# The order of experts, the last scatters and the last column half in a two-layer transformer kernel

## The chip, the cores and the metric

The kernel runs on one core of one Trainium2 chip. The metric is the device time of one execution in microseconds (us); times of the kernel before are the median of three runs. Five engines take part: TensorE (PE in the rows, PEld for its weight loads), VectorE (DVE), ScalarE (ACT), GpSimd (POOL) and SyncE (SP), whose queue issues the loads of weights.

## What is computed

Two transformer layers over 256 tokens of width 1024, in fp32. The first has a latent attention and a dense feed-forward part, the second a sparse attention and a mixture of eight experts. The change touches the mixture and the last layer norm alone:

```python
def moe_swiglu(x, w_router, w_gate, w_up, w_down):      # cut
    logits = (xt @ w_router).astype(jnp.float32)
    top_val, top_idx = lax.top_k(logits, TOP_K)         # 2 of 8 experts per token
    wts = jax.nn.softmax(top_val, -1)
    ...
        xb = xt[toks]                                   # tokens of expert e
        h = jax.nn.silu(xb @ w_gate[e]) * (xb @ w_up[e])    # 1024 -> 3584
        return (h @ w_down[e]) * wr[:, None]                # 3584 -> 1024
    ...
    y = jnp.zeros_like(xt).at[row_tok].add(out.reshape(R, D))

x = layer_norm(alpha * x + f, ln_ffn_g[i], ln_ffn_b[i])
```

Every expert's three matrices are 3 x 1024 x 3584 fp32 numbers, 44.04 MB; all eight are read, 352 MB.

## The kernel before

**Experts and their order.** Expert 0 of the weights is always done first, since its loads start before the router's choice is known. `arrange()` ranks the other seven by their number of tokens (rank 1 has the most), and the constant `turn` says which rank is done at which place: before, places 0 to 7 take ranks 0, 7, 1, 6, 2, 5, 3, 4. `PLAIN` lists the places that are done plainly: at most 64 tokens, weights used in fp32 as they landed. The other three places, of ranks 1 to 3, take up to 128 tokens; there each weight chunk is split by ScalarE (L128) and VectorE (L131) into a high and a low fp32r part, and each product is three fp32r matmuls. A place with more tokens than its limit has a second pass at the end (L1857 on), which is left out when its counter is zero.

**Steps.** Place 0 has steps of 512, 2048 and 1024 hidden columns, the others of 2048 and 1536. In `run()`, for each step: the gate products (L1622, banks `pa`), the first half of the down products of the step before (L1622, banks `pb`), the up products, and the rest of those down products. Transposes of the hidden rows (L1554), the gathering of the next expert's tokens (L1530) and the scatters of the last expert (L1716, L1717, and the weighted sum into `y` on VectorE, L1719) are put between chunks from a queue `fq`.

**Chunks and buffers.** Weights come in chunks of 1 MiB (0.75 MiB in gate and up steps of 1536 columns), each with one or two DMAs on SyncE's queue, in the order in which they are used. An expert has 42 MiB. `seq()` (L421 on) writes out by hand which buffer each chunk goes to: after the first 22 loads the buffers raw0 to raw4, R0, xTh, xTl, x3Th, xna, s2, x3Tl and lng are taken in rotation. R1 to R4 are in it too, until eight keys before ("mg", 2, 0, 0), the first gate chunk of place 2; then they hold the split parts (`rings`, four half chunks of each part). lng leaves the rotation at ("mg", 7, 0, 0), as it takes the norm's gains then. A load is issued when its buffer's last chunk has been used (plain) or split (the others).

**The end.** Place 7's last two down chunks are cut by output columns, `down_tail(at, 0)` and `down_tail(at, 1)`, each with two DMAs of half a MiB. `end()` does half 0, evacuates its bank with `outs` (ScalarE L482, VectorE L483: a high and a low part), puts the scatters of half 0 into `fq`, does half 1, whose `fill` calls take them from there, evacuates it, and does the rest of scatters, squares (L507), means (L511), gains (L520), roots (L515, L516, GpSimd L493) and outputs (L523), with four output DMAs on SyncE (L1817).

Of the kernel before, what the change touches and what calls it, by code (L numbers as in the profile page):

```python
# [20 lines left out]
E = 8  # L21
FE = 3584
FF = 2816
PLAIN = 0, 1, 3, 5, 7


def body(tc, a, out, tap=None, upto=9):
# [31 lines left out]
    HL, NR = 5, 5  # L59
# [221 lines left out]
    fq = deque()  # L281
# [138 lines left out]
    def seq():  # L420

        at = {f"raw{i}": n for i, n in enumerate((2, 3, 5, 6, 7))}
        at.update({z: first.index(z) for z in ("xTh", "xTl", "xna", "lng", "s2", "x3Tl")})
        at.update({i: first.index(R[i]) for i in range(HL)})

        at["x3Th"] = keys.index(("md", 0, 2, 0))

        until = dict.fromkeys(range(1, HL), keys.index(("mg", 2, 0, 0)) - 8)

        until["lng"] = keys.index(("mg", E - 1, 0, 0))  # L430
        yield from first
        n = len(first)
        while True:
            z = min((z for z in at if n < until.get(z, 9999)), key=at.get)
            at[z] = n
            n += 1
            yield R[z] if z in range(HL) else "raw" if z[:3] == "raw" else z
# [76 lines left out]
    def ln_rstd(sm):  # L514
        dve.tensor_scalar(sm[:, 7:8], sm[:, 3:4], sm[:, 4:5], 1.0 / D, op0=ALU.add, op1=ALU.mult)  # L515
        dve.tensor_scalar(sm[:, 7:8], sm[:, 7:8], sm[:, 6:7], LN_EPS, op0=ALU.subtract, op1=ALU.add)  # L516
        rpow(sm[:, 8:9], sm[:, 7:8])
# [53 lines left out]
    p = pT()  # L571
# [1124 lines left out]
    def down_tail(at, i):  # L1696

        e, j, G, hT, acc, gen = at
        key = "md", e, j, i, "tail"
        w = raw_of(*key)  # L1700
        for m in range(2):
            for q in range(2):
                mm(acc[i][64 * q:64 * q + 64], hT[m - 2][:, 64 * q:64 * q + 64], w[2 * m + q], False, m == 1)
            fill(2)
        used(*key)

    def outs(acc, hf):
        oo = four(F32R)
        oo = oo[:, :512], oo[:, 512:]
        evac2(*oo, acc[hf])  # L1710
        return oo

    def scatter(e, oo, ohT, hf, t, sums=None):
        c = slice(hf * 512, hf * 512 + 512)
        p = pT()
        pe.matmul(p, ohT[:, t, :], oo[hf][0], start=True, stop=False)  # L1716
        pe.matmul(p, ohT[:, t, :], oo[hf][1], start=False, stop=True)  # L1717
        y = ys[0]
        dve.scalar_tensor_tensor(y[:, t, c], p, by[0][:, 2 + t, e:e + 1], y[:, t, c], op0=ALU.mult, op1=ALU.add,  # L1719
                                 accum_out=sums[t][:, hf:hf + 1] if sums is not None else None)  # L1720

    def run(todo, G, at, gen=(), end=None):


        nxt, acc = None, None
        for n, (e, base) in enumerate(todo):
            ss = widths(e, gen)
            for j, (c0, wd) in enumerate(ss):
                last_j = j == len(ss) - 1
                final = last_j and n == len(todo) - 1  # L1730
                if last_j and not final:
                    nxt, th = gather(*todo[n + 1])
                    th[0]()
                g = first_gate(G) if (e, j, gen) == (0, 0, ()) else gate_up("mg", e, j, G, gen)
                fill(99)
                if len(order) == 1:
                    arrange()
                elif (e, j, gen) == (0, 2, ()):
                    y = ep.tile([128, 2, D], F32, tag="y", name="y")
                    ys.append(y)  # L1740
                    for t in range(2):
                        scale(y, t)
                elif (e, j, gen) == (E - 1, 0, ()):
                    gains()
                hh = hidden_tile()
                for z, p in each_bank(hh, g):
                    act.activation(z, p, AF.Silu)  # L1747
                m = 0
                if at is not None:
                    if at[1] == 0:  # L1750
                        acc = [pB(), pB()]
                    at = (*at[:4], acc, gen)
                    m = widths(at[0], gen)[at[1]][1] // 256
                    down(at, range((m + 1) // 2))
                if last_j and not final:
                    fq.extend(th[1:])
                u = gate_up("mu", e, j, G, gen)
                fill(99)
                for z, p in each_bank(hh, u):
                    dve.tensor_tensor(z, z, p, op=ALU.mult)  # L1760
                hT, ths = hid_T(hh, wd, G["plain"])
                if final:
                    now(ths[:0])
                    down(at, range((m + 1) // 2, (m + 1) // 2 + 1))
                    now(ths)
                    down(at, range((m + 1) // 2 + 1, m))
                else:
                    down(at, range((m + 1) // 2, m)) if at is not None else None
                    if at is not None and at[0] != e:
                        scatters(at)  # L1770
                    fq.extend(ths)
                at = (e, j, G, hT)
            if nxt is not None:
                G = nxt
        at = (*at, acc, gen)
        m = wd // 256
        if end is not None:
            down(at, range(m - 2))
            oo = []
            end(lambda hf: down_tail(at, hf), lambda hf: oo.append(outs(acc, hf)),  # L1780
                lambda hf, t, sums: scatter(e, oo, G["ohT"], hf, t, sums))
            return
        down(at, range(m))
        scatters(at)
        fill(99)
# [26 lines left out]
    def n_gain(t, hf, z):  # L1812
        ln_gain(sums[t], ys[0][:, t, :], z[:, t, :], lng[0], hf)
# [5 lines left out]
    def norm_rest(z):  # L1819
        n_gain(0, 1, z)  # L1820
        ln_rstd(sums[0])
        ln_mean(sums[1])
        n_gain(1, 0, z)
        for i in range(2):
            n_out(0, i, z)
        ln_rstd(sums[1])
        n_gain(1, 1, z)
        for i in range(2):
            n_out(1, i, z)
# [4 lines left out]
    def end(dn, ev_, sc):  # L1834
        scr, z = norm_tiles()
        dn(0)
        ev_(0)
        fq.extend([lambda: None, lambda: (sc(0, 0, sums), n_square(0, 0, scr)), lambda: sc(0, 1, sums)])
        dn(1)
        ev_(1)  # L1840
        n_square(1, 0, scr)
        sc(1, 0, sums)
        n_square(0, 1, scr)
        sc(1, 1, sums)
        ln_mean(sums[0])
        n_square(1, 1, scr)
        n_gain(0, 0, z)
        norm_rest(z)
# [32 lines left out]
def constants():  # L1881
    import numpy as np
    c = {}
    i = np.arange(128)
    c["ident"] = np.eye(128)
    c["tri"] = np.concatenate([np.zeros((128, 128)), np.where(i[None, :] > i[:, None], NEG, 0.0)], 1)
    c["utri"] = (i[:, None] < i[None, :]).astype(np.float64)
    c["iota"] = np.tile(np.arange(320.0), (128, 1))
    e = np.arange(8)
    c["jlt"] = np.tile((e[None, :] < e[:, None]).astype(np.float64).reshape(1, 64), (128, 1))  # L1890
    n = np.arange(16)
    cm = [((128 * t + i[:, None]) >= 16 * n[None, :] + 31) & (n[None, :] < 15) for t in range(2)]
    c["cmask"] = np.concatenate(cm, 1)
    freq = np.power(np.float32(10000.0), -np.arange(32, dtype=np.float32) / np.float32(32))
    ang = np.arange(256, dtype=np.float32)[:, None] * freq[None, :]
    lay = lambda z: np.concatenate([z[:128], z[128:]], 1)
    c["cos"], c["sin"] = lay(np.cos(ang)), lay(np.sin(ang))
    c["nsin"] = -c["sin"]
    c["tie"] = np.tile(np.where(e == 0, 1e6, -e.astype(np.float64)), (128, 1))
    c["turn"] = np.tile(np.array([0.0, 7, 1, 6, 2, 5, 3, 4]), (128, 1))  # L1900
    c["most"] = np.tile(np.where(np.isin(e, PLAIN), 64.0, 128.0), (128, 1))
    packed = np.concatenate([c[k].astype(np.float32) for k, _ in CONST_COLS], 1)
    assert packed.shape[1] == sum(n for _, n in CONST_COLS)
    idx = np.arange(384)
    dist = 255 - idx
    nn = np.maximum(dist, 0)
    nf = np.maximum(nn, 1).astype(np.float32)
    large = 16 + (np.log(nf / np.float32(16)) / np.float32(math.log(8.0)) * np.float32(16)).astype(np.int32)
    bk = np.where(nn < 16, nn, np.minimum(large, 31))
    oh = np.zeros((33, 384), np.float32)  # L1910
    oh[np.where(dist < 0, 32, bk), 383 - idx] = 1.0
    return {"consts": np.ascontiguousarray(packed), "bucket": oh}
# [26 lines left out]
```

## Time and profile before

| | us |
|---|---|
| median of three runs | 1328.43 (1328.12 to 1332.17) |
| the profiled execution | 1331.11 |
| its span, first to last instruction | 1329.3 |
| TensorE busy | 1293.7 (97%) |
| VectorE busy | 719.6 (54%) |
| ScalarE busy | 594.6 (45%) |
| HBM read | 427 MB, 322 GB/s over the span |

The page cuts the span into 40 slices of 33.2 us; the mixture takes the slices from the fifteenth on. A busy TensorE is not TensorE at its peak, as ends of matmuls are modelled; the idle time and the granted clock tell more. Times within the trace are from the span's start.

### The profile page before, as it was taken

What the parts mean: (1) busy time and instruction counts of PE and PEld (TensorE: products, weight loads), DVE (VectorE), ACT (ScalarE), POOL (GpSimd) and SP (SyncE); (2) the same over time, 40 slices, a digit from 0 to 9 for tenths busy, and PEclk for the clock granted to TensorE, in tenths of its full rate; (3) what the DMA queues carried; (4) which work ended last, traced back from release to release, by engine and by line L of the source; (5) the groups of instructions that cost most, each with busy time, mean ns of one, the idle gap of its engine ahead of it and who ended that gap; (6) DMA issues with size and microseconds to landing.
All of it is one profiled execution on the core that took longest, in us unless ns stands there. A gap on an engine that the chain in (4) does not pass through costs nothing.

```text
span 1329.3 us, 19696 instructions
## 1 busy us (share of the span) xinstructions
PE 1293.7 (97%) x7391; PEld 922.4 (69%) x7391; DVE 719.6 (54%) x1206; ACT 594.6 (45%) x948; POOL 29.3 (2%) x52
## 2 busy tenths in 40 slices
PE   8999999999999999999999999999999999999994
PEld 7878999989988673433477955466984557895441
DVE  5757545567778760002278753167963247874313
ACT  5544444455477521100266742056753136673201
POOL 0001000002100000000000000000000000000000
PEclk9999999999999999999999999999999999999998
DMA  9635555579622399999999999999999999999993
GB/s 308 224 96 192 165 186 191 190 196 261 192 79 82 126 359 400 416 418 413 420 420 417 419 419 419 417 420 419 417 419 415 417 420 419 418 407 397 379 409 145
DMA packets 129577, 429.52 MB, mean 323 GB/s; under 512 B 12680, under 2 KB 65174, under 8 KB 103233
## 3 DMA queue, kind: packets, MB, share of 16 engines
q1 hardware_dynamic: 127120, 421.03, 81.8%
q0 software_dynamic: 2352, 7.14, 1.8%
q8 instruction: 60, 0.98, 0.3%
q14 instruction: 45, 0.36, 0.1%
HBM read 427.07 MB, written 1.07 MB: 322 GB/s over the span
## 4 chain that ended last, share of the span: by engine, by line
PE 85%; DMA 8%; DVE 4%; ACT 2%; issue 0%; POOL 0%; SPq 0%; DVEq 0%; ACTq 0%; POOLq 0%
PE pa L1622 32%; PE pb L1622 16%; PE pa L267 6%; PE pa L269 5%; PE pa L268 5%; DMA raw<-in_moe_w_up_dram 3%; DMA raw<-in_moe_w_gate_dram 3%; PE pt L1530 2%; PE pb L267 2%; PE pb L268 2%; PE pb L269 2%; PE pt L1554 1%; PE pb L1236 1%; DMA wlo<-in_moe_w_gate_dram 1%; PE pt L267 1%; DVE wlo L131 1%
## 5 line engine op out<-in xcount | busy, mean ns | idle before, releaser
L131 DVE TENSOR_TENSOR wlo<-raw,whi 128x1024 fp32r<-128x1024 f32 (+3 forms) x371 | 418.5, 1147 | 245.0 <-ACT whi L128 237.8
L128 ACT CAST whi<-raw 128x1024 fp32r<-128x1024 f32 (+3 forms) x371 | 361.9, 989 | 266.5 <-PE pa L1622 70.4
L1622 PE MATMUL pa<-whi,xe 128*128 128x512 f32 (+3 forms) x860 | 251.3, 393 | 1.9 <-ACT whi L128 1.7
L1622 PE MATMUL pa<-raw,xe 128*64 128x512 f32 (+2 forms) x1064 | 223.6, 562 | 0.0
L1622 PEld LDWEIGHTS pa<-whi,xe 128*128 128x128 f32 (+1 forms) x860 | 149.3, 183 | 37.9 <-issue 12.9
L1622 PE MATMUL pa<-wlo,xe 128*128 128x512 f32 (+3 forms) x476 | 163.9, 407 | 0.8 <-DVE wlo L131 0.8
L1622 PEld LDWEIGHTS pa<-raw,xe 128*64 128x64 f32 x1064 | 72.4, 134 | 125.9 <-issue 115.0
L1622 PE MATMUL pb<-whi,four 128*128 128x512 f32 (+1 forms) x376 | 126.9, 418 | 0.0
L1622 PE MATMUL pb<-raw,four 128*64 128x512 f32 x480 | 108.0, 594 | 0.3 <-DMA raw<-in_moe_w_down_dram 0.3
L1760 DVE TENSOR_TENSOR hh<-hh,pa 128x512 f32<-128x512 f32 (+2 forms) x44 | 25.4, 616 | 138.6 <-PE pa L1622 130.1
L1622 PEld LDWEIGHTS pa<-wlo,xe 128*128 128x128 f32 (+1 forms) x476 | 79.1, 178 | 22.0 <-issue 11.0
L1622 PEld LDWEIGHTS pb<-whi,four 128*128 128x128 f32 (+1 forms) x376 | 68.6, 183 | 27.7 <-issue 11.0
L1622 PE MATMUL pb<-wlo,four 128*128 128x512 f32 (+1 forms) x208 | 85.0, 434 | 0.0
L1622 PEld LDWEIGHTS pb<-raw,four 128*64 128x64 f32 x480 | 34.2, 136 | 66.0 <-issue 63.4
L267 PE MATMUL pa<-xTh,whi 128*128 128x256 f32 x216 | 67.5, 313 | 0.0
L269 PE MATMUL pa<-xTh,wlo 128*128 128x256 f32 x216 | 61.1, 283 | 0.5 <-DVE wlo L131 0.5
L268 PE MATMUL pa<-xTl,whi 128*128 128x256 f32 x216 | 61.0, 283 | 0.0
L1747 ACT ACTIVATE hh<-pa 128x512 f32<-128x512 f32 (+2 forms) x44 | 21.9, 543 | 74.9 <-PE pa L1622 74.9
L267 PE MATMUL pb<-xTh,whi 128*128 128x256 f32 x176 | 49.9, 284 | 0.0
L268 PE MATMUL pb<-xTl,whi 128*128 128x256 f32 x176 | 49.8, 283 | 0.0
L269 PE MATMUL pb<-xTh,wlo 128*128 128x256 f32 x176 | 49.8, 283 | 0.0
L1622 PEld LDWEIGHTS pb<-wlo,four 128*128 128x128 f32 (+1 forms) x208 | 37.0, 178 | 10.7 <-issue 3.3
(411 smaller groups left out, 1896.7 us busy)
## 6 DMA issues: line engine op xcount, KB each, us to landing
raw<-in_moe_w_down_dram SPq DMA_DIRECT2D x94, 1024.0 KB, 14.9
raw<-in_moe_w_up_dram SPq DMA_DIRECT2D x60, 1024.0 KB, 13.0
raw<-in_moe_w_gate_dram SPq DMA_DIRECT2D x60, 1024.0 KB, 14.8
raw<-in_moe_w_up_dram SPq DMA_DIRECT2D x52, 768.0 KB, 13.5
raw<-in_moe_w_gate_dram SPq DMA_DIRECT2D x51, 768.0 KB, 15.0
raw<-in_nsa_w_in_dram SPq DMA_DIRECT2D x23, 512.0 KB, 7.2
raw<-in_ffn_w_gate_dram SPq DMA_DIRECT2D x11, 1024.0 KB, 5.4
raw<-in_ffn_w_up_dram SPq DMA_DIRECT2D x11, 1024.0 KB, 5.3
```

The lines of the kernel that those rows point to most:

```text
L128: act.copy(hi[:, :h], src)
L131: (pool if later == "pool" else dve).tensor_tensor(lo[:, :h], src, f(hi[:, :h]), op=ALU.subtract)
L267: pe.matmul(o, lh, rh, start=first, stop=False)
L268: pe.matmul(o, lh, rl, start=False, stop=False)
L269: pe.matmul(o, ll, rh, start=False, stop=last)
L1236: pe.matmul(p[:, :2 * nk].rearrange("p (b n) -> p b n", b=2), qT[:, i, t * 128:(t + 1) * 128], kswT[:, g, :, :nk], start=True, stop=True)
L1530: pe.matmul(p[:, i * m:i * m + m], x3[:, t, k * 128:(k + 1) * 128], f(G["oh"][:, t, :m]), start=t == 0, stop=t == 1)
L1554: pe.transpose(p[:, (c - c0) * 128:(c - c0 + 1) * 128], hh[:, c * 128:c * 128 + 128] if plain else hh[:, o:o + 255:2], ident)
L1622: pe.matmul(o, l, r, start=first, stop=last, skip_group_check=True)
L1747: act.activation(z, p, AF.Silu)
L1760: dve.tensor_tensor(z, z, p, op=ALU.mult)
```

## The change

- `turn` becomes 0, 1, 7, 2, 6, 3, 5, 4 and `PLAIN` 0, 2, 4, 6, 7: the three places that split are 1, 3 and 5 in place of 2, 4 and 6, and places 6 and 7 are both plain. Each rank keeps its way of being done.
- R1 to R4 leave the rotation eight keys before ("mg", 1, 0, 0), one expert earlier.
- `end()` puts no scatter into `fq`: both halves of the last down product are done and evacuated, then come the four scatters.
- Half 1 is evacuated by `outs_plain`: one fp32 copy, 256 columns on ScalarE and 256 on VectorE. Its scatters are one fp32 matmul in place of two fp32r ones.
- In `norm_rest` the second `ln_rstd` (two steps on VectorE and one on GpSimd) comes ahead of the first two outputs.

```diff
-PLAIN = 0, 1, 3, 5, 7
+PLAIN = 0, 2, 4, 6, 7
...
-        until = dict.fromkeys(range(1, HL), keys.index(("mg", 2, 0, 0)) - 8)
+        until = dict.fromkeys(range(1, HL), keys.index(("mg", 1, 0, 0)) - 8)
...
+    def outs_plain(acc, hf):
+
+        oo = four()[:, :512]
+        act.copy(oo[:, :256], acc[hf][:, :256])
+        dve.tensor_copy(oo[:, 256:], acc[hf][:, 256:])
+        return oo,
+
     def scatter(e, oo, ohT, hf, t, sums=None):
...
-        pe.matmul(p, ohT[:, t, :], oo[hf][0], start=True, stop=False)
-        pe.matmul(p, ohT[:, t, :], oo[hf][1], start=False, stop=True)
+        if len(oo[hf]) == 1:
+            pe.matmul(p, f(ohT[:, t, :]), oo[hf][0], start=True, stop=True)
+        else:
+            pe.matmul(p, ohT[:, t, :], oo[hf][0], start=True, stop=False)
+            pe.matmul(p, ohT[:, t, :], oo[hf][1], start=False, stop=True)
...
-            end(lambda hf: down_tail(at, hf), lambda hf: oo.append(outs(acc, hf)),
+            end(lambda hf: down_tail(at, hf), lambda hf: oo.append((outs_plain if hf else outs)(acc, hf)),
...
         n_gain(1, 0, z)
+        ln_rstd(sums[1])
         for i in range(2):
             n_out(0, i, z)
-        ln_rstd(sums[1])
         n_gain(1, 1, z)
...
         dn(0)
         ev_(0)
-        fq.extend([lambda: None, lambda: (sc(0, 0, sums), n_square(0, 0, scr)), lambda: sc(0, 1, sums)])
         dn(1)
         ev_(1)
-        n_square(1, 0, scr)
+        for t in range(2):
+            sc(0, t, sums)
+            n_square(t, 0, scr)
         sc(1, 0, sums)
...
-    c["turn"] = np.tile(np.array([0.0, 7, 1, 6, 2, 5, 3, 4]), (128, 1))
+    c["turn"] = np.tile(np.array([0.0, 1, 7, 2, 6, 3, 5, 4]), (128, 1))
```

## Rows read from the trace of the kernel before

**Rows 1.** Page: TensorE's share of slices and GB/s, in 40 slices.

```profile
PE   8999999999999999999999999999999999999994
GB/s 308 224 96 192 165 186 191 190 196 261 192 79 82 126 359 400 416 418 413 420 420 417 419 419 419 417 420 419 417 419 415 417 420 419 418 407 397 379 409 145
```

**Rows 2.** Windows by expert: stretch, us, busy us (count) by engine, PEclk, DMA, GB/s.

```profile
573.50:656.20 82.70, 80.72 (x408) 30.65 (x404) 8.04 (x13) 7.13 (x13) 0.00 (x0) 1.00 1.02 416
656.20:780.00 123.80, 122.61 (x594) 99.88 (x596) 98.92 (x103) 83.30 (x97) 0.00 (x0) 0.99 1.02 419
780.00:872.40 92.40, 92.40 (x455) 43.14 (x455) 28.93 (x34) 23.09 (x29) 0.00 (x0) 1.00 1.02 419
872.40:992.60 120.20, 120.20 (x594) 98.62 (x594) 94.73 (x98) 80.38 (x94) 0.00 (x0) 1.00 1.02 419
992.60:1085.10 92.50, 92.50 (x456) 43.21 (x455) 29.84 (x34) 23.10 (x29) 0.00 (x0) 1.00 1.02 417
1085.10:1205.50 120.40, 120.40 (x596) 98.70 (x596) 93.90 (x97) 80.53 (x94) 0.00 (x0) 1.00 1.01 415
1205.50:1310.60 105.10, 104.97 (x493) 46.07 (x494) 25.55 (x31) 20.87 (x28) 0.00 (x0) 1.00 0.94 374
```

**Rows 3.** Windows of 2 us around the third expert's start.

```profile
654.00:656.00 2.00, 0.56 (x4) 0.00 (x0) 0.00 (x0) 0.88 (x1) 0.00 (x0) 1.00 1.04 434
658.00:660.00 2.00, 2.00 (x6) 1.62 (x5) 2.00 (x4) 1.62 (x2) 0.00 (x0) 0.50 1.02 426
```

**Rows 4.** The last chunk's two DMAs (line 82): first and last start, time to landing.

```profile
L82 SPq DMA_DIRECT2D raw<-in_moe_w_down_dram x2: 543/543/543, 1292.0 to 1293.3; - x2
...
DMA to landing us min/median/max: 13.9/13.9/13.9
```

**Rows 5.** Windows in the last expert: after SyncE's pause, to the end, last bytes.

```profile
1239.00:1251.00 12.00, 12.00 (x54) 3.95 (x51) 5.92 (x6) 2.72 (x3) 0.00 (x0) 1.00 0.91 320
1239.00:1310.60 71.60, 71.47 (x351) 30.00 (x348) 16.40 (x22) 8.73 (x12) 0.00 (x0) 1.00 0.92 366
1306.00:1308.00 2.00, 2.00 (x12) 0.57 (x8) 0.00 (x0) 0.33 (x1) 0.00 (x0) 1.00 0.05 19
```

**Rows 6.** Timeline of the end: start, us, engine, line, operation, names, count, [idle before].

```profile
1300.59 7.89 PE L1622 MATMUL pb<-raw,four 128*64 128x512 f32 x36
...
1309.47 1.08 PE L1622 MATMUL pb<-raw,four 128*64 128x512 f32 x4
1309.58 0.75 DVE L1719 SCALAR_TENSOR_TENSOR y<-pt,ordered,y 128x512 f32<-128x512 f32 x1 [0.60 <-PE pt L1717]
1310.48 0.49 PE L1716 MATMUL pt<-four,ohT 128*128 128x512 f32 x1
1311.34 0.56 ACT L482 CAST four<-pb 128x512 fp32r<-128x512 f32 x1
1311.94 0.69 DVE L483 TENSOR_TENSOR four<-pb,four 128x512 fp32r<-128x512 f32 x1
...
1314.57 0.21 DVE L511 TENSOR_SCALAR lnst<-lnst 128x1 f32<-128x1 f32 x1
...
1319.49 0.92 POOL L493 TENSOR_TENSOR lnst<-lnst,nhalf 128x1 f32<-128x1 f32 x1 [2.14 <-DVE lnst L516]
1320.45 1.41 DVE L523 SCALAR_TENSOR_TENSOR z<-z,lnst,lng 128x512 f32<-128x512 f32 x2 [0.44 <-POOL lnst L493]
```

**Rows 7.** Chain of waits: three down chunks, small expert and large: start, us.

```profile
923.35 5.30 PE pb L1622 x24
...
1250.18 8.56 PE pb L1622 x36
```

**Rows 8.** Timeline of SyncE's queue: the pause between two issues in the last expert.

```profile
1227.53 0.33 SPq L84 DMA_DIRECT2D wlo<-in_moe_w_gate_dram  x1
1236.30 12.46 SPq L91 DMA_DIRECT2D raw<-in_moe_w_gate_dram  x7
```

**Rows 9.** Window of 2 us ahead of the mixture, TensorE half busy.

```profile
448.00:450.00 2.00, 0.98 (x6) 0.55 (x4) 1.93 (x10) 1.07 (x5) 0.00 (x0) 1.00 0.26 41
```

## The prediction

> **Names.** A *small* expert (in PLAIN) takes its weights as they landed: a chunk of 1 MiB costs TensorE eight recorded matmuls, and its buffer is free when they are done. A *large* expert's chunk is first split by ScalarE and VectorE into two parts and then costs twelve matmuls; its buffer is free after the split, up to two chunks ahead of TensorE. Both bring 42 MiB (44.04 MB) from HBM. Order before: S S L S L S L S; after: S L S L S L S S.
>
> **What bounds the kernel now.** I read the page first: TensorE is 97% busy and the transfers run near 417 GB/s from the seventeenth slice on, so neither row tells which of the two is late [rows 1]. The windows cut at the first gate product of each expert do [rows 2]. Large stages take 120.2 and 120.4 us, small ones 92.4 and 92.5, TensorE without a gap. At 417 GB/s 44.04 MB take 105.6 us. So the transfers gain on TensorE in a large stage and lose in a small one, and what counts is the **lead**: bytes moved less bytes used.
>
> It can be read from the end backwards. At 1205.5, where the last expert starts, it and six down chunks of the one before are unused: 48 MiB, 50.33 MB. Moved from there on were 105.1 us x 374 = 39.3 MB, so the lead was 11.0 MB. Stage by stage further back (44.04 MB used, us x GB/s moved) it was 5.1 MB at 1085.1, 10.5 at 992.6, 4.2 at 872.4, 9.6 at 780.0, 1.7 at 656.2; over the second small expert, which used 40 MiB (41.9 MB), 9.3 at 573.5 [rows 2]. Two small experts at the front take the lead almost to nothing, and there alone TensorE starves: busy 0.56 of the 2 us from 654, and at 658 to 660 the granted clock is 0.50, its 1.2 GHz level [rows 3]. The stage from 573.5 has 2.0 us of idle in it, the stage from 656.2 1.2 us, and that one is 3.5 us longer than its twins [rows 2]: the starving costs some 5 us. Afterwards TensorE is dense, so the end is TensorE's: the last weights land at 1293.3 + 13.9 = 1307.2 [rows 4], hardly any bytes move from 1306 on [rows 5], and the last down product ends at 1309.47 + 1.08 = 1310.55 [rows 6].
>
> **Part 1: the order of experts.** No product, byte or DMA is added; the three large experts move up by one place. That removes the starving at 654. What it does to the lead:
> - Start of the second expert: 573.5, lead 9.3 MB, as before. The edit of `until` hands R1 to R4 to the split copies earlier; three loads of the first expert (into R2, R3, R4) go into later buffers. A thinner lead there is refilled in the large stage that follows, so I cost it at nothing; uncovered it is at most 3 MiB, 7.5 us.
> - Second expert, now large: 120.3 us less two small down chunks (its predecessor's last step has four, not six; three take 5.30 us [rows 7], so 3.5), 116.8 us. Moved 48.7 MB, used 41.9: the lead would be 16.1 MB.
> - That doesn't fit. How much fits is shown where SyncE stands still: after 1227.53 no issue until 1236.30 [rows 8], and then only 320 GB/s from 1239 to 1251 [rows 5]. At 1239 35 chunks, 36.7 MB, were unused and 71.6 us x 366 = 26.2 MB still to move [rows 5]: lead 10.5 MB, 2.1 below the twelve buffers then in rotation (12.6 MB). Until the last expert's first key `lng` is a thirteenth: 11.6 MB in a small expert, and up to two split chunks more, 13.7, at the end of a large one. So the transfers stop for 2.4 to 4.5 MB, 6 to 11 us, in the second expert, which later stages would have to pay back.
> - Then small some -5.4, large some +6.2 MB [rows 2]: each large stage ends at or near the limit again. At the start of the seventh expert the lead is 11.6 to 13.7 MB; what is over 11.6 stops the issues while TensorE drains it. I take 12.1, nearer to the measured stall.
> - That start is 573.5 + 116.8 + 92.45 + 120.3 + 92.45 + 120.3 = 1115.8.
> - From there two small experts and six chunks: 90 MiB, 94.37 MB; to be moved 82.3 MB. The stage with small after small ran at 416 GB/s [rows 2]: 197.8 us, to 1313.6; a landing comes about 1 us after the last bytes [rows 4, 5]: **1314.6**, against 1307.2.
> - TensorE alone would need 92.45 us, then 105.1 less 6.5 (six small down chunks, 10.6 us, for six large, 17.1 [rows 7]) less 1.0 (part 2): to 1305.9. The end is now the transfers'.
>
> The starving is thus not removed but put to the end, where nothing behind it makes up for it. Four matmuls (1.08 us [rows 6]) follow the last half chunk: last product over at 1315.7, **5.1 us later** than 1310.55.
>
> The Trainium skill ("SBUF — State Buffer", section "Summary: rules for kernel authors") says to reckon with some 358 GB/s between HBM and SBUF. By that the 82.3 MB would take 230 us, and the sum would be 32 us worse; the rows, with 415 to 419 GB/s, contradict it here.
>
> **Part 2: scatters after all down products.** Before, TensorE did the first scatter between the halves of the last down product: 1300.59 + 7.89 = 1308.48 to 1309.47 [rows 6], so 1.0 us is won if TensorE is the bound. If the last bytes are, it is worth nothing: that scatter lay under the wait. Cost: one of four scatter sums on VectorE ran ahead of 1310.55; now all come behind. A scatter pair (0.49) and the step to VectorE, 0.6; four sums of 0.75, and by an estimate 0.6 of small steps: 4.2 us to the first mean, against 1314.57 - 1310.55 = 4.0 [rows 6]. **+0.2 us.**
>
> **Part 3: the last half unsplit.** ScalarE's cast (0.56), then VectorE's difference (0.69) [rows 6] become two half-width copies side by side: up to 0.7 us earlier, but VectorE's chain of sums is what is late, so I take nothing. The scatter's two fp32r products become one of fp32, by a small expert's pair (7.89 us for eighteen) 0.44 us and, over the full array, at most the double; now 0.49 to 0.6. It hides behind the 0.75 of the sum before it; without that cover it costs up to 0.4 twice. Parts 2 and 3 together: -0.7 to +1.0.
>
> **Part 4: both roots ahead of outputs.** VectorE idles 0.44 us ahead of the last two outputs, for GpSimd's second root (0.92 us) [rows 6]. Issued ahead of the first two outputs (1.4 us of VectorE) it is hidden: **-0.44 us**. Those two outputs' DMAs go out on SyncE some 0.5 us later, the last not; the end is behind the last.
>
> **Sum.** +5.1 + 0.2 - 0.44 = +4.8 us. The profiled execution took 1331.11 (span 1329.3); the median of the three runs is 1328.43, 2.7 lower. I put the difference on the median: **1333.2 us**.
>
> **Rivals.**
> *A. More lead fits.* All of 13.7 MB counts and the rate is 419: 80.7 MB, 192.5 us, landed 1309.3, products over at 1310.4: -0.1 - 0.2, 1328.1; half way 1330.6. For it: splits free buffers two chunks ahead. Against: the stall at 1227 came with 10.5 MB.
> *B. Faster: the starving is just gone.* With 15.6 MB of lead at 1115.8 the last half lands at 1304.8, TensorE is dense to 1305.9: -4.65 - 0.24, 1323.5. It decides at fifteen chunks; thirteen and two split ones are just that, but no row shows over 11.0 MB.
> *C. TensorE's clock falls in the last expert.* It would wait some 0.5 us ahead of each chunk there, 70 to 75% busy. Busy 0.98 of 2 us at 448 kept the full clock [rows 9]; the wait at 654 brought it to 0.50 [rows 3]. Half the clock adds 1.1 us to the last four matmuls and up to 2 to the scatters: 1335.5. The Trainium skill ("TensorE: Matmul & The Clock Gate", section "HAM oscillation — how this bites in real kernels") tells of short bursts between DMA waits that are throttled anew each time; by that C would be the likeliest.
>
> **Chances.** Forecast 0.56 (own range 1330 to 1337), A 0.22, B 0.08, C 0.14. About 0.3%, 4 us, is what a measurement here can tell from no change. Faster: B, 0.08. Within: A and a third of the forecast, 0.40. Slower: the rest, 0.52. Range: from 1 us under A's end, 1327, to the forecast with a lead of 10.5 and 415 GB/s (202.1 us, +9.5 - 0.2), rounded up a little, 1338.
>
> **What would show it.** Right: TensorE dense from 502 to about 1270, no low clock at 658; fewer GB/s between 640 and 700, with SyncE waiting for buffers; waits on DMA ahead of the last expert's chunks; full transfers to some 1313, the last product 2 us behind. Wrong: the last landing before 1309, or no waits of TensorE after 1208. Tail: 4.2 us from the last product to the first mean, no idle of VectorE ahead of the last outputs.

## The result and the profile after

The changed kernel takes 1336.51 us (median of seven runs, 1335.24 to 1339.43), the kernel before, run beside it, 1330.13 (seven runs, 1328.12 to 1332.17). The ratio is 1.0052, interval 1.0040 to 1.0064: 6.4 us slower. The forecast was 4.8 us slower. The profiled execution is one of 1336.51 us with a span of 1334.7, 5.4 more than before.

The page of the changed kernel, TensorE's share and the GB/s in 40 slices (33.4 us each), against [rows 1]:

```profile
PE   8999999999999999999999999999999999999985
...
GB/s 312 218 95 191 173 177 188 190 195 271 193 68 94 124 385 409 379 420 389 370 363 418 418 421 417 418 418 397 417 420 421 416 419 392 417 418 420 418 418 187
```

The dips have moved. Before, the transfers ran without a break from slice 17 to 35 and sagged in the last expert (407, 397, 379, 409 GB/s). Now they sag in the slices 17, 19 to 21, 28 and 34 (379; 389, 370, 363; 397; 392), the last two where a small expert follows a large one, and run at full rate from there to the end.

Windows of the changed kernel, cut at the first gate product of each expert: stretch, us, then busy us (count) of PE, PEld, DVE, ACT and POOL, granted clock, DMA share, GB/s. They answer to [rows 2]:

```profile
572.10:688.80 116.70, 116.70 (x577) 97.24 (x576) 93.50 (x96) 80.81 (x94) 0.00 (x0) 1.00 0.99 389
688.80:781.40 92.60, 92.60 (x455) 42.79 (x454) 29.83 (x34) 23.10 (x29) 0.00 (x0) 1.00 1.00 408
781.40:901.80 120.40, 120.40 (x594) 98.56 (x592) 94.13 (x97) 80.82 (x94) 0.00 (x0) 1.00 1.02 418
901.80:994.40 92.60, 92.60 (x455) 42.77 (x454) 29.83 (x34) 23.00 (x29) 0.00 (x0) 1.00 1.01 411
994.40:1114.80 120.40, 120.40 (x596) 98.66 (x594) 94.11 (x97) 80.84 (x94) 0.00 (x0) 1.00 1.02 418
1114.80:1207.10 92.30, 92.30 (x457) 43.28 (x458) 23.91 (x28) 18.58 (x25) 0.00 (x0) 1.00 1.01 409
1207.10:1317.30 110.20, 100.86 (x463) 33.53 (x460) 8.91 (x14) 8.07 (x15) 0.00 (x0) 1.00 0.99 404
```

TensorE has no idle time in the first six stages, where before the second and third lost some. The last stage is 110.2 us long with 100.86 busy: 9.3 us of waiting, nearly all of it new. Two groups in the list of waits (us in total, times, longest; from 500 us on) say for what:

```profile
PE pb L1622 <- DMA raw<-in_moe_w_down_dram: 6.9, 13, 1.0
...
PE pa L1622 <- DMA raw<-in_moe_w_up_dram: 2.5, 6, 0.9
```

The same bookkeeping as in the prediction (weights unused at 1207.1 less bytes moved from there, then back stage by stage) gives the **lead** at the expert starts: 8.3 MB at 572.1, 11.8 at 688.8, 5.5 at 781.4, 11.8 at 901.8, 5.8 at 994.4, 12.1 at 1114.8 and 5.8 at 1207.1. At none of these starts does it exceed 12.1 MB.

The end of the changed kernel, timeline (start, us, engine, line, operation, names, count, idle before), against [rows 6]:

```profile
1310.92 3.74 PE L1622 MATMUL pb<-raw,four 128*64 128x512 f32 x16 [0.63 <-DMA raw<-in_moe_w_down_dram]
1314.83 1.08 PE L1622 MATMUL pb<-raw,four 128*64 128x512 f32 x4 [0.17 <-DMA raw<-in_moe_w_down_dram]
1316.13 1.08 PE L1622 MATMUL pb<-raw,four 128*64 128x512 f32 x4 [0.22 <-DMA raw<-in_moe_w_down_dram]
...
1318.00 0.74 DVE L1729 SCALAR_TENSOR_TENSOR y<-pt,ordered,y 128x512 f32<-128x512 f32 x1
1318.90 1.95 PE L1724 MATMUL pt<-four,ohT 128*128 128x512 f32 x4 [0.56 <-DVE y L1729]
1320.04 0.75 DVE L1729 SCALAR_TENSOR_TENSOR y<-pt,ordered,y 128x512 f32<-128x512 f32 x1 [0.24 <-PE pt L1724]
1321.57 0.21 DVE L511 TENSOR_SCALAR lnst<-lnst 128x1 f32<-128x1 f32 x1
...
1326.93 1.41 DVE L523 SCALAR_TENSOR_TENSOR z<-z,lnst,lng 128x512 f32<-128x512 f32 x2
```

Nearly every group of down products now waits for a DMA; the last begins at 1316.13 and ends at 1317.21. The last outputs (L523) no longer have an idle time ahead of them. The last chunk's two DMAs, against [rows 4], say when its last half landed, at 1303.4 + 12.7 = 1316.1:

```profile
L82 SPq DMA_DIRECT2D raw<-in_moe_w_down_dram x2: 544/694/843, 1300.9 to 1303.4; - x2
...
DMA to landing us min/median/max: 12.7/13.3/13.9
```

**Where the 5.4 us came from.** One thing has to be set aside first: in every trace the mixture's first up product starts at another time, from 499.1 to 504.0 us, by a difference that arises ahead of the mixture; here it starts at 500.52, before at 502.08. Reckoned from it, the last landing came at 805.1 before and 815.6 after, the last down product ended at 808.5 and 816.7. So: -1.56 ahead of the mixture, **+8.2** to the last down product, +0.34 from there to the first mean (4.02, now 4.36), -0.52 from the mean to the end of the last output (7.29, now 6.77), -1.08 from there to the end of the span (7.48, now 6.40). The last figure ranges from 5.7 to 7.6 over all kernels run here; the part on the prediction comes back to it. The sum is +5.4.

In the experiments below, all times are counted from that first up product. "Seventh start" is the first gate product of the seventh expert, "last product" the end of the last down product, "end" the end of the span. Before: seventh start 583.0, last landing 805.1, last product 808.5, end 827.3. After: 614.2, 815.6, 816.7, 834.2.

### The profile page after: what moved, and what is told of

Read it like the earlier page. It is cut to its first block, busy times and chain, and to the rows that moved or that the text cites. A ratio compares the mean times of both kernels' runs of the same rounds, so it can differ in the third digit from the quotient of the medians.

```text
span 1334.7 us, 19668 instructions
## 1 busy us (share of the span) xinstructions
PE 1295.2 (97%) x7391; PEld 918.1 (69%) x7391; DVE 720.2 (54%) x1206; ACT 595.6 (45%) x948; POOL 29.3 (2%) x52
## 4 chain that ended last, share of the span: by engine, by line
PE 88%; DMA 6%; DVE 4%; ACT 1%; issue 0%; POOL 0%; SPq 0%; DVEq 0%; ACTq 0%
PE pa L1622 35%; PE pb L1622 16%; PE pa L267 6%; PE pa L269 5%; PE pa L268 5%; DMA raw<-in_moe_w_down_dram 3%; PE pt L1530 2%; PE pb L267 2%; PE pb L268 2%; PE pb L269 2%; PE pt L1554 1%; PE pb L1236 1%; DMA whi<-in_moe_w_gate_dram 1%; PE pt L267 1%; PE pt L269 1%; PE pt L268 1%
## 5 line engine op out<-in xcount | busy, mean ns | idle before, releaser
L131 DVE TENSOR_TENSOR wlo<-raw,whi 128x1024 fp32r<-128x1024 f32 (+3 forms) x359 | 407.2, 1152 | 209.6 <-ACT whi L128 203.7
L128 ACT CAST whi<-raw 128x1024 fp32r<-128x1024 f32 (+3 forms) x359 | 353.0, 994 | 231.4 <-PE pa L1622 70.7
L1622 PE MATMUL pa<-raw,xe 128*64 128x512 f32 (+2 forms) x1144 | 240.0, 564 | 2.5 <-DMA raw<-in_moe_w_up_dram 2.5
L1622 PE MATMUL pa<-whi,xe 128*128 128x512 f32 (+3 forms) x820 | 240.5, 383 | 0.0
L1622 PEld LDWEIGHTS pa<-raw,xe 128*64 128x64 f32 x1144 | 76.8, 134 | 141.0 <-issue 121.5
L1622 PE MATMUL pa<-wlo,xe 128*128 128x384 f32 (+3 forms) x436 | 153.4, 390 | 0.0
L1622 PE MATMUL pb<-raw,four 128*64 128x512 f32 x528 | 120.5, 596 | 6.9 <-DMA raw<-in_moe_w_down_dram 6.9
L1622 PE MATMUL pb<-whi,four 128*128 128x512 f32 (+1 forms) x352 | 115.4, 406 | 0.0
L1622 PE MATMUL pb<-wlo,four 128*128 128x512 f32 (+1 forms) x184 | 74.0, 414 | 0.0
L1560 ACT COPY four<-pt 128x512 f32<-128x512 f32 (+1 forms) x11 | 6.2, 563 | 91.6 <-PE pt L1554 91.6
```

What stands on the lines that cost most here:

```text
L128: act.copy(hi[:, :h], src)
L131: (pool if later == "pool" else dve).tensor_tensor(lo[:, :h], src, f(hi[:, :h]), op=ALU.subtract)
L1560: (dve.tensor_copy if c0 else act.copy)(z, p[:, :n * 128])
L1622: pe.matmul(o, l, r, start=first, stop=last, skip_group_check=True)
```

## The experiments

**Theory**: the end has gone from TensorE to the transfers, because two small experts at the end use a lead that the buffers cap at some 12 MB. Against it stood A (more lead fits), B (the starving is only removed), C (a low clock in the last expert).

### The order alone, and the tail alone

The kernel before with only the order changed, `e1_order`:

```diff
-PLAIN = 0, 1, 3, 5, 7
+PLAIN = 0, 2, 4, 6, 7
...
-        until = dict.fromkeys(range(1, HL), keys.index(("mg", 2, 0, 0)) - 8)
+        until = dict.fromkeys(range(1, HL), keys.index(("mg", 1, 0, 0)) - 8)
...
-    c["turn"] = np.tile(np.array([0.0, 7, 1, 6, 2, 5, 3, 4]), (128, 1))
+    c["turn"] = np.tile(np.array([0.0, 1, 7, 2, 6, 3, 5, 4]), (128, 1))
```

> Kernel before with the new order of experts alone (PLAIN, turn, until); end as before. Theory (the lead is capped by the buffers, the last two small experts use it up, the last landing sets the end): last weights land some 9 us later than before (1316 us), TensorE waits some 9 us in the last expert; the old tail adds 0.8 us for the scatter between the halves and 0.4 us for the second root: 7 to 8 us slower than before, 1 us slower than the changed kernel. Rival (the tail edits, not the order, made it slower): within 1 us of before.

And its complement, the changed kernel with these three lines as before, `e2_tail`:

> The changed kernel with the old order of experts (PLAIN, turn, until as before): the tail edits alone. Theory: TensorE is the bound at the end, the 1.0 us that the scatter took between the halves is won, one more sum on VectorE costs 0.3 us, the roots give 0.4 us: 1 us faster than before (ratio 0.999). Rival: sums that come late cost more than is won, 0 to 1 us slower.

The order alone: 1338.83 us, ratio 1.0063 (1.0048 to 1.0078). The tail edits alone: 1329.62 against 1329.99, ratio 0.9989 (0.9978 to 1.0001). The order carries the whole loss: 8.8 us by the medians, a little more than the 7 to 8 expected. Its end is at 834.4, that of the full change at 834.2, so by the traces the tail edits are worth 0.2 us where the transfers set the end; by the ratios of the two series it is 1.5 us, with intervals that overlap. In the old order they brought the last product from 808.5 to 807.6 and the end from 827.3 to 826.3: 1.0 us. The timeline of the order alone shows why the moved scatter earns nothing there:

```profile
1317.58 0.50 PE L1716 MATMUL pt<-four,ohT 128*128 128x512 f32 x1
...
1318.26 1.08 PE L1622 MATMUL pb<-raw,four 128*64 128x512 f32 x4
```

The first scatter stands between the halves, but the last half chunk landed only at 1317.82, in the middle of it, so it delays the last four matmuls by 0.4 us and not by 1.0.

### The same tail again

To narrow a gain near nothing, the tail alone was timed once more, `e11_tail_again`:

> The tail edits with the old order of experts once more, the same file as in the second run, for a narrower interval. Theory: 1 us faster than before (ratio 0.999). Rival: no difference, an interval around 1.000.

1327.54 against 1329.32, ratio 0.9989 (0.9978 to 0.9999), end at 825.5. Two series of twelve runs give -0.4 and -1.8 us by medians and the same ratio, some 0.1% or 1.5 us; the second interval ends just below 1, the first just above. This is the only version with a median below that of the kernel before, by a gain at the edge of what the runs can tell; its profile shows the same pieces (first mean +0.34, mean to output -0.52, last product earlier).

### Fewer buffers

If the buffers cap the lead, three fewer must cost time in the changed order. In `seq()` of the changed kernel, `e3_fewbuf`:

```diff
+        until.update(dict.fromkeys(("s2", "x3Tl", "x3Th"), keys.index(("mg", 1, 0, 0))))
         yield from first
```

> The changed kernel with three buffers fewer (s2, x3Tl, x3Th leave the rotation at the second expert). Theory: the lead at the start of the seventh expert is 3.1 MB smaller and every MB of it is 2.4 us at the end: last landing 7.5 us later, 13 to 15 us slower than before. Rival (the end is set by the rate of the last transfers or by TensorE's clock, not by the lead): as the changed kernel, 6 us slower than before.

1351.06 us, ratio 1.0155 (1.0134 to 1.0177): 14.6 us slower than the changed kernel and 21.1 slower than the one before, where 13 to 15 were expected. The last landing came 15.2 us later than in the changed kernel, where 7.5 were expected. Its windows by expert, from the third on:

```profile
688.00:780.50 92.50, 92.50 (x455) 43.16 (x454) 24.10 (x28) 20.18 (x27) 0.00 (x0) 1.00 1.01 407
780.50:903.80 123.30, 121.38 (x596) 98.36 (x594) 98.61 (x103) 83.27 (x97) 0.00 (x0) 1.00 1.01 410
...
996.20:1121.50 125.30, 121.89 (x596) 99.62 (x594) 97.52 (x102) 81.98 (x96) 0.00 (x0) 0.99 1.01 406
1121.50:1213.70 92.20, 92.20 (x455) 43.29 (x456) 23.83 (x28) 18.69 (x25) 0.00 (x0) 1.00 1.01 406
1213.70:1331.60 117.90, 102.28 (x463) 32.31 (x459) 8.92 (x14) 8.03 (x14) 0.00 (x0) 1.00 0.99 406
```

The cap shows: counted in whole chunks that have landed and are not used, the lead is, from the third expert on, 8 at the start that follows a large expert and 1 at the start that follows a small one, where the changed kernel has 10 or 11 and 4. The price comes in two halves. From the seventh start to the last product it is 210.2 us in place of 202.5, and the last expert waits 15.6 us in place of 9.3. The other half arises earlier: with one chunk left, two large stages start by starving and take 123.3 and 125.3 us in place of 120.4, and the seventh start is at 621.8, 7.5 late. The expectation had reckoned with the first half alone.

To see whether the old order has slack in the same place, the same line was put into the kernel before, `e9_fewbuf_before`:

> Kernel before with the same three buffers fewer (s2, x3Tl, x3Th leave at the second expert). Theory: with the old order the lead is 1 MiB at 656 us and 8 MiB at the end of large stages, so ten buffers still hold nearly all of it; the last expert loses 2 to 3 MiB of lead of which some 3 us were spare: 3 to 6 us slower than before, against 14.6 in the changed order. Rival (buffers cost as much in either order): 12 to 16 us slower.

1339.57 us, ratio 1.0071 (1.0056 to 1.0086): 9.8 us slower by the medians, between the 3 to 6 expected and the rival's 12 to 16. Large stages take 125.7, 123.1 and 122.1 us, all three start by starving, and the last expert, too, waits (110.5 us, 107.34 busy). The old order loses less (9.8 against 14.6), but it had less to spare than I thought: at the fifth and seventh expert's start 1 chunk is left in place of 3.

### One buffer more

The changed kernel with R1 left in the rotation, and the split copies with three half chunks in place of four, `e5_morebuf`:

```diff
-        until = dict.fromkeys(range(1, HL), keys.index(("mg", 1, 0, 0)) - 8)
+        until = dict.fromkeys(range(2, HL), keys.index(("mg", 1, 0, 0)) - 8)
...
-    free.extend(rings[1:])
+    free.extend(rings[2:])
```

> The changed kernel with a fourteenth buffer: R1 stays in the rotation for the whole mixture, and the split copies get three half chunks in place of four. Theory (buffers cap the lead): the lead at the start of the seventh expert is 1 MiB larger, the last landing 2.5 us earlier: 4 us slower than before. Rival (three half chunks make TensorE wait for splits in large experts): slower than the changed kernel, with waits on ScalarE and VectorE in its large stages.

1339.73 us, ratio 1.0076 (1.0063 to 1.0088): 10 us slower than before where the theory had 4, and some 3 us slower than the changed kernel: the time is the rival's. What the theory forecast of the lead shows all the same, as a part. Two of its large stages and the last two experts:

```profile
783.50:905.90 122.40, 121.33 (x596) 98.33 (x594) 95.73 (x98) 81.94 (x95) 0.00 (x0) 1.00 1.02 415
...
998.40:1120.70 122.30, 121.25 (x594) 98.40 (x592) 95.71 (x98) 81.95 (x95) 0.00 (x0) 1.00 1.01 415
1120.70:1213.00 92.30, 92.30 (x455) 43.34 (x456) 24.28 (x28) 19.01 (x25) 0.00 (x0) 1.00 1.01 408
1213.00:1320.10 107.10, 101.05 (x463) 34.48 (x460) 8.92 (x14) 8.03 (x14) 0.00 (x0) 1.00 0.99 404
```

The lead at the seventh start is 12 landed chunks in place of 10 (11 in `e1_order` and `e10_noroots`, which have the same order and buffers), and from the seventh start to the last landing there are 198.2 us in place of 201.3: one buffer is worth 3.1 us at the end, near the 2.5 that 1 MiB takes at 417 GB/s. But each large stage is 2 us longer, 1.1 of it idle, with waits of TensorE for split parts (VectorE's `wlo`); the seventh start is 5.8 us late by that, more than the gain.

The same two lines in the kernel with only the tail edits, where TensorE sets the end, `e8_tailr1`:

> The tail edits with the old order of experts, and R1 kept in the rotation as a fourteenth buffer. Theory: the stall of SyncE's queue at 1227 to 1236 us goes, the last landing comes up to 2 us earlier, TensorE's wait of 0.9 us for the last half chunks goes: 1 us faster than the tail edits alone, 2 to 2.5 us faster than before. Rival (split copies too few): waits in the large stages, 2 to 5 us slower than before.

1332.24 us, ratio 1.0020 (1.0011 to 1.0030), 0.0031 above the tail alone; the end is at 829.5 against 826.3. The rival held: the last landing came not 2 us earlier but 3.0 later (808.5 against 805.4). The large stages take 125.0, 122.3 and 122.2 us against 123.8, 120.2 and 120.4 [rows 2], and more lead (10 and 11 chunks at the sixth and eighth start in place of 8 and 9) buys nothing where the end is TensorE's.

### Less work for TensorE

The sharpest question to the theory: if the last landing sets the end, work taken from TensorE in the last expert is worth nothing. `e4_lesspe` is the changed kernel without the up products of six of the eight chunks in the last expert's first step; all loads stay.

```diff
-                    for q in range(2):
+                    for q in range(0 if (which, e, j) == ("mu", E - 1, 0) and 0 < k < 7 else 2):
```

> The changed kernel with six of eight chunks of products left out in the first up step of the last expert (their loads stay): 10 us less work on TensorE. Theory (the last landing sets the end): within 1.5 us of the changed kernel, 5 to 7 us slower than before. Rival (TensorE, by its work or by a lower clock between waits, sets the end): 8 to 10 us faster than the changed kernel, 2 to 4 us faster than before.

1336.55 us, ratio 1.0054 (1.0034 to 1.0073), the same as the changed kernel; end at 833.7 against 834.2. The last two stages:

```profile
1113.90:1206.20 92.30, 92.30 (x457) 43.27 (x458) 23.91 (x28) 18.59 (x25) 0.00 (x0) 1.00 1.01 408
1206.20:1316.00 109.80, 92.24 (x415) 30.55 (x411) 8.92 (x14) 8.04 (x14) 0.00 (x0) 0.95 0.99 406
```

TensorE is busy 8.6 us less, and the stage is 0.4 us shorter: the work went into waiting. Its longest wait, 8.58 us from 1233.3, is a stretch in which TensorE has nothing, and it also brings the clock down, shown by windows of 4 us:

```profile
1232.00:1236.00 4.00, 1.34 (x6) 0.66 (x4) 0.00 (x0) 0.59 (x1) 0.00 (x0) 1.00 1.01 422
1236.00:1240.00 4.00, 0.00 (x0) 0.00 (x0) 0.00 (x0) 0.00 (x0) 0.00 (x0) 0.53 0.99 414
1240.00:1244.00 4.00, 2.07 (x6) 0.76 (x8) 0.00 (x0) 0.00 (x0) 0.00 (x0) 0.50 1.02 424
```

### The edit of the buffers' key, the last half, the roots

The kernel before with only the line of `until`, `e6_until`:

> Kernel before with the edit of until alone: R1 to R4 leave the rotation one expert earlier, though the splits begin with the third. Theory (the lead of the second expert is far below what thirteen buffers hold, so four fewer don't matter): within 1 us of before. Rival (loads of the first expert wait for later buffers and the lead at 573 us shrinks): up to 3 MiB less lead, TensorE starves longer at 654 us, up to 7 us slower.

1330.32 against 1329.78, ratio 1.0006 (0.9997 to 1.0015), end at 827.2 as before. At the second expert's start 7 chunks have landed in place of 8. By the medians the theory holds, but in the trace that chunk isn't free in the old order; the second expert's stage, against the first line of [rows 2]:

```profile
570.50:655.70 85.20, 81.81 (x409) 30.86 (x405) 8.11 (x14) 7.21 (x13) 0.00 (x0) 1.00 1.02 419
```

It is 2.5 us longer, with 3.4 us of starving in place of 2.0, and the last product comes at 810.1 in place of 808.5. The end is the same only because the time behind the last output is 5.8 us here and 7.5 before. In the changed order the large second expert has no idle time (116.70 us, all busy), so no row shows that the edit costs anything there.

The changed kernel with the last half split as the first, `e7_split`:

```diff
-            end(lambda hf: down_tail(at, hf), lambda hf: oo.append((outs_plain if hf else outs)(acc, hf)),
+            end(lambda hf: down_tail(at, hf), lambda hf: oo.append(outs(acc, hf)),
```

> The changed kernel with the last column half evacuated and scattered in two fp32r parts, as before. Theory (VectorE's chain of sums is what is late behind the last product): VectorE's difference (0.69 us) stands ahead of the four sums in place of a copy of 0.42, and waits for ScalarE's full-width cast (0.56): the first mean 0.5 to 1 us later behind the last product than the 4.36 us of the changed kernel. Rival (the one fp32 product, 0.97 us by the trace, is the slower way): first mean earlier than 4.36 us.

A single execution: 1334.71 us, end at 833.7. From the last product to the first mean 4.38 us, with the unsplit half 4.36: it is worth nothing. Its timeline:

```profile
1315.52 0.59 ACT L482 CAST four<-pb 128x512 fp32r<-128x512 f32 x1 [1.95 <-PE pb L1622]
1316.14 0.69 DVE L483 TENSOR_TENSOR four<-pb,four 128x512 fp32r<-128x512 f32 x1 [1.85 <-ACT four L482]
1316.75 0.74 DVE L1729 SCALAR_TENSOR_TENSOR y<-pt,ordered,y 128x512 f32<-128x512 f32 x1
```

The cast and the difference are done ahead of VectorE's first sum (1316.75), and all four sums then follow without a wait for a product. In the changed kernel the two evacuating copies end 0.5 us earlier, but the third sum waits 0.24 us for its fp32 product (1318.90, L1724, above). What is won ahead of VectorE's sums is lost between them. I had expected 0.5 to 1 us here.

The changed kernel with the second root back behind the first two outputs, `e10_noroots`:

```diff
-        ln_rstd(sums[1])
         for i in range(2):
             n_out(0, i, z)
+        ln_rstd(sums[1])
```

> The changed kernel with the second root behind the first two outputs, as before. Theory: VectorE idles 0.4 us again ahead of the last two outputs, from the first mean to the last output's end 7.2 us in place of 6.8. Rival (hidden anyway): no idle, 6.8 us.

A single execution: 1337.6 us, first mean to last output 7.29 us in place of 6.77. The idle time is back, of the same length as in [rows 6]:

```profile
1326.84 0.92 POOL L493 TENSOR_TENSOR lnst<-lnst,nhalf 128x1 f32<-128x1 f32 x1 [2.14 <-DVE lnst L516]
1327.79 1.41 DVE L523 SCALAR_TENSOR_TENSOR z<-z,lnst,lng 128x512 f32<-128x512 f32 x2 [0.44 <-POOL lnst L493]
```

## Why the prediction was right, and where it was off

**The bound.** Right. The last expert's waits are on DMA, full transfers run to the end, and 8.6 us less of TensorE's work changed nothing (`e4_lesspe`).

**Part 1, the order.** The steps held closely. Predicted seventh start 613.7 us behind the first up product (1115.8 less 502.08), measured 614.2; predicted lead there 12.1 MB, measured 12.1 (luck to the last digit, as 12.1 was picked from 11.6 to 13.7 and the other two such starts show 11.8); second expert 116.8 us, measured 116.7. The starving was reckoned at some 5 us. From the second expert's start to the last's, the stages sum to 632.0 us before and 635.0 after, and the new sum holds six small down chunks for six large less at its end, 6.5 us more left in it: 632.0 + 6.5 - 635.0 = 3.5 us. Its disappearance is real and worth nothing, as the lead it stood for is missing at the end.

**The term that was mis-sized** is the transfer time of the last two experts. 82.3 MB were forecast and moved, but in 201.3 us, at 409 GB/s, and not in 197.8 + 1.0 at 416. The rate fell at the seventh expert's start, as windows of the changed kernel show:

```profile
1114.80:1120.00 5.20, 5.20 (x26) 2.13 (x26) 1.29 (x2) 1.07 (x2) 0.00 (x0) 1.00 0.98 383
1120.00:1130.00 10.00, 10.00 (x46) 3.46 (x48) 5.32 (x5) 4.37 (x5) 0.00 (x0) 1.00 0.97 354
1130.00:1140.00 10.00, 10.00 (x44) 6.97 (x40) 2.45 (x2) 3.50 (x5) 0.00 (x0) 1.00 1.00 408
```

Against 416 that is 5.2 x 33 + 10 x 62 + 10 x 8 kB/us, 0.87 MB, 2.1 us. With the 2.5 us that the whole stretch was too long and 0.5 us of a later start, the last landing came 3.1 us later than forecast (815.6 for 812.5), and the last product 8.2 us later than before in place of 5.1. The prediction had named the reason, "what is over 11.6 stops the issues while TensorE drains it", and had then counted all of 12.1 MB at full rate. A lead at its cap is to be taken together with the pause that it brings: 12.1 less 0.87 gives 11.2 MB.

**The cap** was read from one pause of SyncE in the kernel before, and held: 11.8, 11.8 and 12.1 MB at the three ends of large stages. The dip between 640 and 700 was there too (343 GB/s from 640 to 660).

**Part 2.** Right but for small change. Moving the scatter was taken at nothing where the last bytes set the end; in `e1_order` the old scatter made the last four matmuls begin 0.4 us after the landing, in the changed kernel they begin with it. First mean +0.34 where +0.2 stood. In the old order, where TensorE sets the end, the last product came 0.9 us earlier in `e2_tail` (and 1.6 in `e11_tail_again`) where 1.0 stood. **Part 3.** Taken at nothing, and nothing it is (`e7_split`), though one fp32 product took 0.97 us (two take 1.95 at 1318.90) and not 0.44 to 0.88. **Part 4.** -0.44 forecast, -0.52 in the trace and back in `e10_noroots`.

**A** fell: no start of an expert shows over 12.1 MB, and `e5_morebuf` had to add a buffer to get more. **B** fell with it, as it needed 15.6 MB. **C** did not come. TensorE waits 0.2 to 1.0 us ahead of nearly every chunk, and its granted clock stays at full, 2.4 GHz, as two windows of the last expert in the changed kernel show:

```profile
1284.00:1288.00 4.00, 3.38 (x20) 1.10 (x18) 0.00 (x0) 0.00 (x0) 0.00 (x0) 1.00 1.01 416
...
1300.00:1304.00 4.00, 2.81 (x14) 0.84 (x14) 0.00 (x0) 0.00 (x0) 0.00 (x0) 1.00 1.00 415
```

The Trainium skill ("TensorE: Matmul & The Clock Gate", section "HAM oscillation — how this bites in real kernels") tells of a kernel whose bursts between DMA waits are throttled anew each time; there each burst is shorter than the wait behind it. Here the waits are the shorter part (up to 1.0 us, between bursts of 1.1 us and more), so the prediction took more from the page than its case gives. The 8.58 us of `e4_lesspe`, after which the clock was at 0.50, agree with it.

The low clock can come in a last expert, though: in `e9_fewbuf_before` one wait of 1.95 us there was followed by it (the wait, then a window of 2 us):

```profile
1312.52 7.93 PE L1623 MATMUL pb<-raw,four 128*64 128x512 f32 x28 [1.95 <-DMA raw<-in_moe_w_down_dram]
...
1314.00:1316.00 2.00, 2.00 (x8) 0.48 (x6) 0.00 (x0) 0.00 (x0) 0.00 (x0) 0.50 1.05 388
```

**From the profile to the median.** The sum by the pieces is +5.4 on the profiled executions. Of it, -1.6 is the start of the mixture and goes with no edit; +7.0 is left from there on. The medians' +6.4 (interval 5.3 to 8.5) agree with that.

The start differs mostly by the granted clock. Near 115 us, and again near 487 us, TensorE has short waits (1.5, 1.0 and 0.7 us between 480 and 487, the same in both kernels), and behind them the clock fell to 0.50 in some executions and not in others: in the kernel before at both places, in the changed kernel at the first alone. Windows from 488 us, before and after:

```profile
488.00:490.00 2.00, 2.00 (x10) 1.49 (x9) 0.00 (x0) 0.29 (x1) 0.00 (x0) 0.50 1.00 414
...
488.00:490.00 2.00, 2.00 (x14) 1.48 (x12) 0.23 (x2) 0.36 (x1) 0.00 (x0) 1.00 1.01 418
```

Five traces without such a fall start the mixture at 499.1 to 499.7 us, three with one fall at 500.5 to 501.5, five with two at 502.1 to 504.0 (in one of these the second came near 385 us). It does not go with the program: `e2_tail` and `e11_tail_again` are one file, the first with two falls and a start at 504.0, the second with none and 499.4.

The -1.1 behind the last output looks less like chance. It is 7.5 or 7.6 us in the three traces with the old order and its buffers (two of them of one file), 6.3 to 6.6 in the five with the new order and its buffers, 5.7 to 7.2 in the others. The prediction put it at nothing. So the forecast's +4.8 lacked 3.1 us of the landing, and 1.1 us that it had not reckoned took back a third of that: that it came as near as it did is in part luck.

Open: what sets the 5.7 to 7.6 us behind the last output, and why `e2_tail` lost 1.7 us more than the others in its first 20 us. No experiment went into either.

## What to carry to other kernels

Where phases that are bound by transfers alternate with phases that are bound by the matrix engine, keep account of bytes landed less bytes used, phase by phase, and of the cap that the buffers put on it: a phase bound by transfers is hidden only as far as the lead ahead of it goes, and at the end of the kernel nothing makes up for it. Two transfer-bound phases in a row cost 3.5 us of starving at the front here and 9.3 us of waiting at the end. A lead read at its cap is gross, for the queue stands still there: subtract the bytes that the pause leaves unmoved.

## What the hardware showed that I had not expected

A TensorE that is 70 to 94% busy with waits of up to 1.0 us ahead of nearly every chunk kept its full clock for 50 us (windows of 4 us, 1264 to 1316). One wait of 8.58 us brought it to 0.50, and it was still there (0.50) in the 4 us in which work began again; behind one of 1.95 us it fell too (`e9_fewbuf_before`). Behind the same waits ahead of the mixture it fell in one execution and not in another, and that moves the start of the mixture by 1 to 3 us.

One buffer of 1 MiB was worth 3.1 us in a stretch of 200 us that is bound by transfers (`e5_morebuf`). The half chunk of split parts that it displaced cost 2 us in every large stage, although VectorE is idle for a fifth of such a stage and ScalarE for a third.
